# A group's token rows by PE transposes instead of a DRAM round trip, gate stores on ACT's queue, row numbers in one transfer

## The chip, the cores and the metric

The kernel runs on one core of one Trainium2 chip. The metric is the device time of one execution in microseconds (us). PE is the matrix engine, PEld its weight load, DVE the vector engine, ACT the activation engine, POOL the general one. SP only issues transfers. Transfers are issued on the queues of SP, ACT and POOL, and 16 DMA engines carry them all.

## The reference

One layer of a decoder for 256 prompt tokens and 8 sample tokens, D_MODEL = 2048, in float32. Two mixers (a state-space scan and a short convolution) and a layer norm give x1. Then comes a layer of single-neuron experts, 8 heads with the best 16 of 16384 each, a second norm and a gated sum.

```python
def peer(x, w_q, keys1, keys2, u_tab, v_tab):
    ...
    t1, i1 = lax.top_k(s1, PEER_TOPK)
    t2, i2 = lax.top_k(s2, PEER_TOPK)
    ...
    top, pos = lax.top_k(cand, PEER_TOPK)
    idx = jnp.take_along_axis(cand_idx, pos, axis=-1)
    gate = jax.nn.softmax(top, axis=-1)
    ...
        hid = jax.nn.gelu(jnp.einsum('td,thkd->thk', xb, u_tab[ib]).astype(jnp.float32), approximate=False)
        coef = (gb * hid).astype(xb.dtype)
        return jnp.einsum('thk,thkd->td', coef, v_tab[ib])
```

## The kernel before

All activations lie transposed (features on partitions, 264 tokens along the free dimension). Weights stream in halves of a 128-column block (128x1024, 512 KB). SP fetches a half into one of five w buffers (L135), ACT rounds it to whi (L146), DVE takes the rest as wlo (L147), and PE multiplies with both. `next_half` runs the fetch four halves and the split three halves (LOOK = 3) ahead of PE.

The program order is made by a tick after every half. `tick` calls `background`, which runs the functions that `defer` and `soon` have made due and then lets the tasks (generators) issue work up to a budget; a task yields the DVE time it has issued, or ("w", n) to rest n ticks. On the chip each engine and each queue takes its instructions in that order.

After the first norm (x1) and the queries, the experts are done in two ways.

- **208 tokens, dense.** All 16384 experts are multiplied with them on PE: the U stage (`pair_block` with uT, 128 blocks, results evacuated by L1350, L1351, L1354 and stored to a_d on ACT's queue, L1355) and the V stage (vP). `select` (DVE) finds each token's experts. `gates` makes one-hot tiles (L1218 on POOL and DVE, L1219 and L1220 on ACT). `g_mm` multiplies them on PE (L1231), ACT copies the result into gs (L1232), and every 32 tokens gs is stored to g_d (2 MB, 7 stores, the last into gr_d half as long) on SP's queue (L1223). The V stage reads g_d and a_d back.
- **56 tokens, sparse** (x1sp: 48 of the prompt and the 8 of the samples), by gathering the rows of the chosen experts. They are in three groups, GR = 32, 16 and 8 tokens. A tile of 128 partitions holds, for each of its chosen experts, one row of 2048. For group g it has 128/n experts of each of n tokens at a time, so the token's x1 must stand on its 128/n partitions: the tile x1s.

`send` (L1172 on) writes the chosen indices (ix) and gates (sel) to sx_d and sg_d in DRAM, in an order that `index` (L1263, L1264) can read as one column per gather. Prompt tokens (t = 0) go on POOL's queue, 16 transfers of the samples (t = 1) on SP's queue, two ticks after they are made (`later_rows`). `token_rows` transposes the 56 tokens on PE (16 transposes, L1242), copies them out (L1243) and stores each group's rows with 128/n copies to x1_d in DRAM (L1246, 3 stores of 1 MB on POOL's queue, x_d in the profile). `replicate` (L1268) reads a group's 128 rows back into x1s.

`sparse_experts` then runs 112 jobs on a grid of ticks. Each gathers 128 rows (ug, 1 MB, L1257 on POOL) and works on them on DVE: a product with x1s and its sum for uR (L1307), or a weighted sum into x1s for vR (L1317). `folded` sums the partitions of one token by a matmul with the 0/1 matrix fld.

Of the kernel before, what the change touches and what calls it, by code (L numbers as in the profile page):

```python
# [17 lines left out]
D = 2048  # L18
# [34 lines left out]
def hybrid_step(ctx: ExitStack, tc: tile.TileContext, xT, pT, w_in, w_dt, w_bs, w_bc, w_o, w_q, w_pg, w_pp,  # L53
# [1113 lines left out]

    sx_d = [dram.tile([128, n], U32, name=f"sx{g}_d") for g, (_, n) in enumerate(GR)]
    sg_d = [dram.tile([128, n], F, name=f"sg{g}_d") for g, (_, n) in enumerate(GR)]
    x1_d = [dram.tile([128, D], F, name=f"x1{g}_d") for g in range(len(GR))]  # L1170

    def send(sel, t, nh):  # L1172

        sp = P["sp"]
        ix = sp.tile([128, nh * TOPK], U32, name=f"ix{t}")
        fx = sp.tile([128, nh * TOPK], F, name="fx", tag="fx", bufs=1)
        n = TT[t][1]
        ve.scalar_tensor_tensor(fx[:n], sel[:n, 0], 128.0, sel[:n, 1], OP.mult, OP.add)
        ve.tensor_copy(ix[:n], fx[:n])

        def rows(eng, g, tok, src, stride, runs, m):
            for d, x in ((sx_d[g], ix), (sg_d[g], sel[:, 2])):
                eng.dma_start(out=bass.AP(tensor=d.tensor, offset=d.offset + tok * m,
                                          ap=[[m, len(src)], [stride, runs], [1, m]]),
                             in_=x[src.start:src.stop].rearrange("p (c m) -> p c m", m=m))

        if t == 0:
            for g, (k0, m) in enumerate(GR):
                lo = n - (NSP - NS) + k0
                src = range(lo, min(lo + m, n))  # L1190
                if len(src):
                    rows(gp, g, 0, src, m * m, 128 // m, m)
        else:
            g, m = len(GR) - 1, GR[-1][1]

            def later_rows():
                for h in range(PH):
                    rows(sy, g, h * TOPK + m - NS, range(h * NS, h * NS + NS), m * m, TOPK // m, m)
                DONE["sent"] = True

            defer(2, later_rows)
# [3 lines left out]
    def gates(t0, n):  # L1205
        oh = P["oh"]
        grid = Grid()
        for tt in range(t0, t0 + n, 4):
# [13 lines left out]
            if q0 + 4 == tb:  # L1222
                defer(8, lambda gs=gs, b0=b0: sy.dma_start(out=g_d[b0] if b0 < NB else gr_d, in_=gs))  # L1223
# [9 lines left out]

    def token_rows():

        while "x1" not in DONE or later:
            yield ("w", 1)
        xr = lp.tile([128, D], F, name="xr", tag="ug", bufs=2)
        for b in range(4):
            ps = bank("x1t")  # L1240
            for q in range(4):
                te.transpose(ps[:NSP, q * 128:(q + 1) * 128], x1sp[:, 4 * b + q], ident)  # L1242
            ac.copy(xr[:NSP, b * 512:(b + 1) * 512], ps[:NSP])  # L1243
            yield ("w", 1)
        for g, (k0, n) in enumerate(GR):
            gp.dma_start(out=x1_d[g].rearrange("(q n) d -> n q d", n=n),  # L1246
                         in_=xr[k0:k0 + n, None, :].to_broadcast([n, 128 // n, D]))

    def sparse_experts():
# [15 lines left out]

        def replicate(g):
            t = lp.tile([128, D], F, name="x1s", tag="x1s", bufs=2)
            gp.dma_start(out=t, in_=x1_d[g])  # L1268
            return t
# [20 lines left out]
        xr = replicate(0)  # L1290
        yield ("w", 4)
        grid = Grid()
        g = 0
        for i, (tab, k0, n, c) in enumerate(jobs):
            ks = slice(k0, k0 + n)
            if tab is uR and c == k0:
                x1s = xr
            if tab is vR and c == k0 and g + 1 < len(GR):
                while g + 1 == len(GR) - 1 and "sent" not in DONE:
                    yield ("w", 1)  # L1300
                index(g + 1)
                xr = replicate(g + 1)
# [35 lines left out]
    spawn(token_rows())  # L1338
# [223 lines left out]
def _inputs(x_prompt, x_sample, p_prompt, p_sample, state_ssm, state_ssd_conv, state_shortconv,  # L1562
# [35 lines left out]
        fold=np.concatenate([np.tile(np.eye(g[1]), (128 // g[1], 1)) for g in GR], 1).astype(np.float32),  # L1598
# [34 lines left out]
```

## Time and profile before

| what | value |
|---|---|
| three runs | median 2633.68 us, 2633.47 to 2635.28 |
| the profiled execution | 2632.36 us, its span 2630.5 us |
| mean granted clock of PE | 0.993 |
| busy: PE, DVE, ACT, POOL | 98%, 78%, 54%, 24% of the span |
| DMA | 695.29 MB, 264 GB/s over the span |
| DMA queues' share of 16 engines: SP (q1), POOL (q0), ACT (q10) | 58.8%, 16.8%, 2.0% |
| chain that ended last | PE 76%, DMA 9%, DVE 8%, issue 3%, ACT 2% |

The span runs from the first to the last instruction; the time of the execution is 1.9 us longer. PE's busy share is that of modelled ends and overlapping matmuls, so its idle time and its granted clock (1.00 is 2.4 GHz, 0.50 is 1.2 GHz) tell more. The dense blocks of the U stage end between 1147 and 1874 us, those of the V stage between 1878 and 2514.

### The profile page before, as it was taken

To read this page: it belongs to the slowest core of one execution; us is meant where nothing else is said; L and a number is where in the kernel's file an instruction comes from. 1 tells how busy PE (TensorE), PEld (TensorE's weight loads), DVE (VectorE), ACT (ScalarE), POOL (GpSimd) and SP (SyncE) were. 2 spreads that over 40 slices of the span, in tenths; PEclk is the share of its full clock that TensorE was granted. 3 is DMA by queue.
4 is the path that set the end of the run, shared out by engine and by line. 5 is a ranking of instruction groups with operands and counts; after the bars stand their busy time and mean duration, and the time that the engine had idled before them with its cause. 6 is when DMAs were issued, how large, how long until landed. Compare 5 with 4: busy or idle time off the path is not lost.

```text
span 2630.5 us, 49103 instructions
## 1 busy us (share of the span) xinstructions
PE 2572.6 (98%) x18989; PEld 2536.3 (96%) x18989; DVE 2044.0 (78%) x3308; ACT 1425.5 (54%) x2170; POOL 630.5 (24%) x725
## 2 busy tenths in 40 slices
PE   9999999999999999998999999999999999999999
PEld 8999999999999999997989999998999999999999
DVE  8899965556445567897988777677899989989986
ACT  5665533454334445653567777775544444444563
POOL 2232200000000010100148656752222223322210
PEclk9999999999999999999999999999999999999999
DMA  7798755655666665667779999999999999999664
GB/s 237 219 302 272 238 175 177 184 174 182 179 182 180 181 177 178 181 188 197 219 259 347 344 342 353 344 347 382 369 366 358 379 353 364 374 356 371 207 203 132
DMA packets 204378, 695.29 MB, mean 264 GB/s; under 512 B 23616, under 2 KB 61168, under 8 KB 188144
## 3 DMA queue, kind: packets, MB, share of 16 engines
q1 hardware_dynamic: 156512, 509.13, 58.8%
q0 software_dynamic: 29616, 164.98, 16.8%
q10 hardware_dynamic: 18016, 18.06, 2.0%
q8 instruction: 148, 2.42, 0.4%
q14 instruction: 86, 0.70, 0.1%
HBM read 649.46 MB, written 42.61 MB: 263 GB/s over the span
## 4 chain that ended last, share of the span: by engine, by line
PE 76%; DMA 9%; DVE 8%; issue 3%; ACT 2%; POOL 1%; SPq 0%; ACTq 0%; DVEq 0%; POOLq 0%
PE mm L273 18%; PE mm L239 15%; PE mm L237 15%; PE mm L238 15%; PE mm L274 9%; DMA w<-vP 4%; DVE wlo L147 4%; DMA w<-uT 3%; ACT whi L146 1%; PE mm L276 1%; PE gps L1231 1%; POOL o L1218 1%; DVE ug L1307 1%; DVE x1s L1317 1%; DMA ug<-uR,sidx 0%
## 5 line engine op out<-in xcount | busy, mean ns | idle before, releaser
L147 DVE TENSOR_TENSOR wlo<-w,whi 128x1024 fp32r<-128x1024 f32 x916 | 1116.1, 1224 | 441.9 <-ACT whi L146 432.7
L146 ACT CAST whi<-w 128x1024 fp32r<-128x1024 f32 x916 | 958.3, 1049 | 796.2 <-PE mm L238 285.4
L273 PE MATMUL mm<-x,whi 128*128 128x416 f32 x1920 | 604.4, 374 | 14.3 <-ACT whi L146 14.2
L273 PE MATMUL mm<-co,whi 128*128 128x416 f32 x1920 | 587.7, 367 | 0.0
L239 PE MATMUL mm<-x,wlo 128*128 128x264 f32 x1920 | 549.2, 286 | 2.8 <-DVE wlo L147 2.8
L237 PE MATMUL mm<-x,whi 128*128 128x264 f32 x1920 | 549.1, 286 | 0.0
L238 PE MATMUL mm<-x,whi 128*128 128x264 f32 x1920 | 546.6, 285 | 0.0
L274 PE MATMUL mm<-x,wlo 128*128 128x208 f32 x2048 | 518.0, 263 | 20.6 <-DVE wlo L147 20.4
L274 PE MATMUL mm<-co,wlo 128*128 128x208 f32 x2048 | 513.9, 261 | 6.1 <-DVE wlo L147 5.6
L274 PEld LDWEIGHTS mm<-x,wlo 128*128 128x128 f32 x2048 | 396.4, 194 | 30.3 <-DVE wlo L147 29.8
L274 PEld LDWEIGHTS mm<-co,wlo 128*128 128x128 f32 x2048 | 390.4, 191 | 12.5 <-DVE wlo L147 11.8
L273 PEld LDWEIGHTS mm<-x,whi 128*128 128x128 f32 x1920 | 366.9, 191 | 20.9 <-ACT whi L146 16.1
L239 PEld LDWEIGHTS mm<-x,wlo 128*128 128x128 f32 x1920 | 361.8, 188 | 3.3 <-DVE wlo L147 3.2
L273 PEld LDWEIGHTS mm<-co,whi 128*128 128x128 f32 x1920 | 360.9, 188 | 3.6 <-ACT whi L146 0.2
L237 PEld LDWEIGHTS mm<-x,whi 128*128 128x128 f32 x1920 | 362.6, 189 | 1.5 <-issue 1.4
L238 PEld LDWEIGHTS mm<-x,whi 128*128 128x128 f32 x1920 | 362.9, 189 | 0.0
L1218 POOL TENSOR_SCALAR o<-iot,slot,slot 128x128 f32<-128x128 f32 x156 | 213.9, 1377 | 5.8 <-issue 2.9
L1257 POOL DMA_INDIRECT ug<-vR,sidx x56 | 99.2, 1771 | 318.1 <-DVE x1s L1317 268.3
L1257 POOL DMA_INDIRECT ug<-uR,sidx x56 | 92.9, 1660 | 271.5 <-DVE ug L1307 232.2
L1307 DVE SCALAR_TENSOR_TENSOR ug<-ug,x1s 128x2048 f32<-128x2048 f32 x56 | 127.9, 2283 | 3.6 <-DMA ug<-uR,sidx 3.6
L1317 DVE SCALAR_TENSOR_TENSOR x1s<-ug,scf,x1s 128x2048 f32<-128x2048 f32 x53 | 124.3, 2345 | 4.9 <-DMA ug<-vR,sidx 4.9
L840 POOL CAST r1h<-r1gbh 128x2 fp32r<-128x2 f32 x16 | 5.2, 325 | 476.2 <-PE mm L239 476.2
(363 smaller groups left out, 3928.1 us busy)
## 6 DMA issues: line engine op xcount, KB each, us to landing
w<-uT SPq DMA_DIRECT2D x256, 512.0 KB
w<-vP SPq DMA_DIRECT2D x256, 512.0 KB
w<-w_in SPq DMA_DIRECT2D x240, 512.0 KB
w<-w_bc SPq DMA_DIRECT2D x32, 512.0 KB
w<-w_bs SPq DMA_DIRECT2D x32, 512.0 KB
w<-w_o SPq DMA_DIRECT2D x32, 512.0 KB
w<-w_q SPq DMA_DIRECT2D x32, 512.0 KB
w<-w_pg SPq DMA_DIRECT2D x32, 512.0 KB
```

What stands on the lines that cost most here:

```text
L146: ac.copy(hi, w)
L147: ve.tensor_tensor(lo, w, hi.bitcast(F), OP.subtract)
L237: te.matmul(ps, wh, xh[kb], start=(first and q == 0), stop=False)
L238: te.matmul(ps, wh, xl[kb], start=False, stop=False)
L239: te.matmul(ps, wl, xh[kb], start=False, stop=(last and q == n - 1))
L273: te.matmul(ps, hi[:, ws], xp[kb], start=(kb == 0), stop=False)
L274: te.matmul(ps[:, :TD], lo[:, ws], xp[kb][:, :TD], start=False, stop=False)
L276: te.matmul(ps, hi[:, ws], xp[kb], start=False, stop=True)
L1218: (gp if q < 3 else ve).tensor_scalar(o1[:, q], iot, slot[0][:, c], slot[2][:, c], OP.is_equal, OP.mult)
L1257: gp.indirect_dma_start(out=t, out_offset=None, in_=tab, in_offset=bass.IndirectOffsetOnAxis(ap=sidx[:, c:c + 1], axis=0))
L1307: ve.scalar_tensor_tensor(t, t, 1.0, x1s, OP.mult, OP.mult, accum_out=shid[:, c:c + 1])
L1317: ve.scalar_tensor_tensor(x1s, t, scf[:, c:c + 1], x1s, OP.mult, OP.add)
```

## The change

- `token_rows` and x1_d are gone. `replicate` becomes a task: for each quarter of the 2048 features it spreads the group's columns of x1sp on ACT over 128 columns (each token 128/n times; in the last group by one copy for each of 8 heads), rests a tick, transposes the four 128x128 blocks on PE, copies them out on ACT and rests a tick. The first group waits for it; the next ones are spawned where `replicate` was called.
- The order of a group's partitions follows (token first), and the fold matrix with it. The row numbers and gates of a group are written to DRAM as they stand, by one transfer each, all on POOL's queue; the samples' are written when they are made.
- Gate stores go on ACT's queue.

```diff
--- before.py
+++ after.py
@@ -1165,9 +1165,9 @@
         yield from gates(0, PT // 2)
 
 
+
     sx_d = [dram.tile([128, n], U32, name=f"sx{g}_d") for g, (_, n) in enumerate(GR)]
     sg_d = [dram.tile([128, n], F, name=f"sg{g}_d") for g, (_, n) in enumerate(GR)]
-    x1_d = [dram.tile([128, D], F, name=f"x1{g}_d") for g in range(len(GR))]
 
     def send(sel, t, nh):
 
@@ -1178,27 +1178,16 @@
         ve.scalar_tensor_tensor(fx[:n], sel[:n, 0], 128.0, sel[:n, 1], OP.mult, OP.add)
         ve.tensor_copy(ix[:n], fx[:n])
 
-        def rows(eng, g, tok, src, stride, runs, m):
+        for g, (k0, m) in enumerate(GR):
+            if (g + 1 == len(GR)) != (t == 1):
+                continue
+            lo = 0 if t else n - (NSP - NS) + k0
             for d, x in ((sx_d[g], ix), (sg_d[g], sel[:, 2])):
-                eng.dma_start(out=bass.AP(tensor=d.tensor, offset=d.offset + tok * m,
-                                          ap=[[m, len(src)], [stride, runs], [1, m]]),
-                             in_=x[src.start:src.stop].rearrange("p (c m) -> p c m", m=m))
-
-        if t == 0:
-            for g, (k0, m) in enumerate(GR):
-                lo = n - (NSP - NS) + k0
-                src = range(lo, min(lo + m, n))
-                if len(src):
-                    rows(gp, g, 0, src, m * m, 128 // m, m)
-        else:
-            g, m = len(GR) - 1, GR[-1][1]
-
-            def later_rows():
-                for h in range(PH):
-                    rows(sy, g, h * TOPK + m - NS, range(h * NS, h * NS + NS), m * m, TOPK // m, m)
-                DONE["sent"] = True
-
-            defer(2, later_rows)
+                x = x[lo:lo + (n if t else m)]
+                gp.dma_start(out=bass.AP(tensor=d.tensor, offset=d.offset, ap=[[x.shape[1], x.shape[0]], [1, x.shape[1]]]),
+                             in_=x)
+        if t:
+            DONE["sent"] = True
 
     GS = {}
 
@@ -1220,7 +1209,7 @@
             ac.activation(o2, o2, AF.Relu, bias=1.0, scale=-1.0)
             defer(6, lambda o1=o1, o2=o2, gs=gs, q0=q0: g_mm(o1, o2, gs, q0))
             if q0 + 4 == tb:
-                defer(8, lambda gs=gs, b0=b0: sy.dma_start(out=g_d[b0] if b0 < NB else gr_d, in_=gs))
+                defer(8, lambda gs=gs, b0=b0: ac.dma_start(out=g_d[b0] if b0 < NB else gr_d, in_=gs))
             yield 0.1
             yield grid(3)
         DONE["G" + str(t0)] = True
@@ -1230,21 +1219,6 @@
         for q in range(4):
             te.matmul(ps[:, q * 128:(q + 1) * 128], o2[:, q], o1[:, q], start=True, stop=True)
         ac.copy(gs[:, :, q0:q0 + 4].rearrange("p e t -> p t e"), ps.rearrange("p (t e) -> p t e", e=128))
-
-    def token_rows():
-
-        while "x1" not in DONE or later:
-            yield ("w", 1)
-        xr = lp.tile([128, D], F, name="xr", tag="ug", bufs=2)
-        for b in range(4):
-            ps = bank("x1t")
-            for q in range(4):
-                te.transpose(ps[:NSP, q * 128:(q + 1) * 128], x1sp[:, 4 * b + q], ident)
-            ac.copy(xr[:NSP, b * 512:(b + 1) * 512], ps[:NSP])
-            yield ("w", 1)
-        for g, (k0, n) in enumerate(GR):
-            gp.dma_start(out=x1_d[g].rearrange("(q n) d -> n q d", n=n),
-                         in_=xr[k0:k0 + n, None, :].to_broadcast([n, 128 // n, D]))
 
     def sparse_experts():
         jobs = [(tab, k0, n, c) for k0, n in GR for tab in (uR, vR) for c in range(k0, k0 + n)]
@@ -1263,10 +1237,29 @@
             gp.dma_start(out=sidx[:, k0:k0 + n], in_=sx_d[g])
             gp.dma_start(out=scf[:, k0:k0 + n], in_=sg_d[g])
 
+        XR = {}
+
         def replicate(g):
+
+            k0, n = GR[g]
             t = lp.tile([128, D], F, name="x1s", tag="x1s", bufs=2)
-            gp.dma_start(out=t, in_=x1_d[g])
-            return t
+            for b in range(4):
+                tb = t[:, b * 512:(b + 1) * 512]
+                x = x1sp[:, 4 * b:4 * b + 4, k0:k0 + n]
+                if g + 1 < len(GR):
+                    ac.copy(tb.rearrange("p (q i c) -> p q i c", q=4, i=n),
+                            x[:, :, :, None].to_broadcast([128, 4, n, 128 // n]))
+                else:
+                    for h in range(PH):
+                        ac.copy(tb.rearrange("p (q h i c) -> p q h i c", q=4, h=PH, i=NS)[:, :, h],
+                                x[:, :, :, None].to_broadcast([128, 4, n, TOPK // NS]))
+                yield ("w", 1)
+                ps = bank("x1t")
+                for q in range(4):
+                    te.transpose(ps[:, q * 128:(q + 1) * 128], tb[:, q * 128:(q + 1) * 128], ident)
+                ac.copy(tb, ps)
+                yield ("w", 1)
+            XR[g] = t
 
         def folded(g, acc):
 
@@ -1287,19 +1280,18 @@
         yield ("w", 1)
         index(0)
         get(0)
-        xr = replicate(0)
-        yield ("w", 4)
+        yield from replicate(0)
         grid = Grid()
         g = 0
         for i, (tab, k0, n, c) in enumerate(jobs):
             ks = slice(k0, k0 + n)
             if tab is uR and c == k0:
-                x1s = xr
+                x1s = XR.pop(g)
             if tab is vR and c == k0 and g + 1 < len(GR):
                 while g + 1 == len(GR) - 1 and "sent" not in DONE:
                     yield ("w", 1)
                 index(g + 1)
-                xr = replicate(g + 1)
+                spawn(replicate(g + 1))
             get(i + 1)
             yield grid(STEP - (i % (4 if vp else 2) == 0))
             t = rows.pop(i)
@@ -1335,7 +1327,6 @@
     ctx.push(sp_stack)
     ctx.push(oh_stack)
     slot = [tp.tile([128, TD], F, name=f"slot{q}") for q in range(3)]
-    spawn(token_rows())
     spawn(select_all())
 
 
@@ -1595,7 +1586,8 @@
         eye=np.eye(128, dtype=np.float32),
         tri=np.triu(np.ones((128, 128), np.float32)),
         iota=np.tile(np.arange(128, dtype=np.float32), (128, 1)),
-        fold=np.concatenate([np.tile(np.eye(g[1]), (128 // g[1], 1)) for g in GR], 1).astype(np.float32),
+        fold=np.concatenate([np.repeat(np.eye(n), 128 // n, 0) for _, n in GR[:-1]]
+                            + [np.tile(np.repeat(np.eye(NS), TOPK // NS, 0), (PH, 1))], 1).astype(np.float32),
     )
```

**SP's queue.** Before, with the weights w counted where they follow each other; these are the last two of the samples' sixteen transfers and the first gate stores (one piece of the difference):

```order
-L1183 DMA sx_d<-ix_16283 8x2x8
-L1183 DMA sg_d<-sel_16075 8x2x8
-L135 DMA w<-uT 128x1024 x24
-L1223 DMA g_d<-gs 128x4096
-L135 DMA w<-uT 128x1024 x22
-L1223 DMA g_d<-gs 128x4096
-L135 DMA w<-uT 128x1024 x13
-L1223 DMA gr_d<-gs 128x2048
-L135 DMA w<-uT 128x1024 x25
```

All of it is gone: the 256 uT weights now stand in one row, with nothing between them.

**POOL**, from the keys' loads to the first gather (o are the one-hots of a gate). Before:

```order
L1013 DMA keys<-keysT 128x256 x8
L1246 DMA x_d<-xr 32x4x2048
L1246 DMA x_d<-xr 16x8x2048
L1246 DMA x_d<-xr 8x16x2048
L1183 DMA sx_d<-ix_16010 32x4x32
L1183 DMA sg_d<-sel_15353 32x4x32
L1183 DMA sx_d<-ix_16010 16x8x16
L1183 DMA sg_d<-sel_15353 16x8x16
L1218 TENSOR_SCALAR o_16105<-iot,slot_14375,slot_14377 128x128 x3
```

Now:

```order
L1013 DMA keys<-keysT 128x256 x8
L1187 DMA sx_d<-ix_15979 32x128
L1187 DMA sg_d<-sel_15322 32x128
L1187 DMA sx_d<-ix_15979 16x128
L1187 DMA sg_d<-sel_15322 16x128
L1207 TENSOR_SCALAR o_16074<-iot,slot_14372,slot_14374 128x128 x3
L1207 TENSOR_SCALAR o_16182<-iot,slot_14372,slot_14374 128x128 x3
L1187 DMA sx_d<-ix_16252 64x16
L1187 DMA sg_d<-sel_16044 64x16
L1207 TENSOR_SCALAR o_16295<-iot,slot_14372,slot_14374 128x128 x3
```

The three stores of token rows are gone, and the samples' two transfers stand between the second and the third gate.

**ACT** in the U stage, at the first group's second quarter, as it is now (in as the hidden values of the dense experts are made):

```order
L1341 COPY as<-mm 128x208
L1221 COPY gs<-gps 128x4x128
L1250 COPY x1s<-x1sp 128x512
L1208 ACTIVATE o_16413<-iot,slot_14373 128x128 x4
L1209 ACTIVATE o_16413<-o_16413 128x512
L146 CAST whi<-w 128x1024
L1345 ACTIVATE as<-as 128x416
L1346 DMA a_d<-as 128x416
L1260 COPY x1s<-x1t 128x512
L146 CAST whi<-w 128x1024
```

The spreading copy and the copy out of PSUM are new there, each between two casts of weights; the four transposes stand on PE between them.

## Rows read from the trace of the kernel before

**Rows 1.** The page: busy us of each engine (share of the span) xinstructions.
```profile
PE 2572.6 (98%) x18989; PEld 2536.3 (96%) x18989; DVE 2044.0 (78%) x3308; ACT 1425.5 (54%) x2170; POOL 630.5 (24%) x725
```

**Rows 2.** Stretches: us, busy (xinstructions) of PE PEld DVE ACT POOL, PEclk, DMA share, GB/s.
```profile
1210.00:1220.00 10.00, 10.00 (x70) 9.88 (x70) 9.65 (x33) 5.71 (x8) 1.74 (x3) 1.00 0.91 210
1225.00:1280.00 55.00, 39.90 (x206) 36.28 (x204) 36.07 (x102) 17.55 (x24) 0.00 (x0) 0.81 0.71 198
1330.00:1345.00 15.00, 11.95 (x61) 11.16 (x60) 8.75 (x31) 8.20 (x17) 4.12 (x5) 0.77 0.91 344
1345.00:1370.00 25.00, 22.60 (x156) 22.15 (x155) 23.70 (x63) 18.45 (x31) 4.92 (x4) 1.00 0.66 209
```

**Rows 3.** PE's timeline: start, us, line, operation; in brackets the idle time before.
```profile
1229.29 0.37 PE L273 MATMUL mm<-x,whi 128*128 128x416 f32 x1
...
1234.25 0.71 PE L273 MATMUL mm<-x,whi 128*128 128x416 f32 x1 [4.18 <-ACT whi L146]
...
1235.85 0.59 PE L273 MATMUL mm<-x,whi 128*128 128x416 f32 x1
```

**Rows 4.** DMA, 1210 to 1250: queue, packets, MB, share of 16 engines; issues.
```profile
q0 software_dynamic: 560, 3.15, 50.9%
...
x_d<-xr POOLq DMA_DIRECT2D x3, 1024.0 KB
```

**Rows 5.** Chain of waits, 1165 to 1360: start, us, what.
```profile
1219.53 29.39 DMA w<-uT
```

**Rows 6.** Stretches, columns as in rows 2: selection stage, and before it.
```profile
1223.62:1367.03 143.41, 122.86 (x745) 117.68 (x744) 112.69 (x288) 75.36 (x120) 25.45 (x26) 0.90 0.72 219
1193.14:1223.62 30.48, 30.48 (x208) 29.87 (x208) 29.03 (x98) 16.65 (x25) 1.74 (x3) 1.00 0.78 190
```

**Rows 7.** SP's timeline, 1300 to 1420: first small transfer, next weight.
```profile
1326.17 0.35 SPq L1183 DMA_DIRECT2D sx_d<-ix  x1
...
1336.54 56.36 SPq L135 DMA_DIRECT2D w<-uT  x24
```

**Rows 8.** SP's waits, whole span: us in total, times, longest.
```profile
SPq L1223 <- ACT gs L1232: 22.4, 5, 6.0
...
SPq L1223 <- ACT as L1354: 10.5, 2, 6.0
...
SPq L1183 <- DVE ix L1179: 5.0, 1, 5.0
```

**Rows 9.** Stretches behind the seven gate stores: first, last, sum (columns of rows 2).
```profile
1400.00:1430.00 30.00, 27.05 (x185) 26.29 (x184) 22.09 (x30) 20.91 (x36) 19.71 (x16) 1.00 0.95 357
...
1780.00:1810.00 30.00, 28.01 (x174) 26.96 (x172) 19.78 (x20) 15.35 (x24) 7.64 (x9) 0.94 1.01 398
sum 160.00, PE 149.72 PEld 143.77 DVE 114.62 ACT 111.90 POOL 78.02; mean PE 21.39 PEld 20.54 DVE 16.37 ACT 15.99 POOL 11.15
```

**Rows 10.** Reads of x1s: its issues (1656 to 1690, then tile); stretches behind.
```profile
x1s<-x_d POOLq DMA_DIRECT2D x1, 1024.0 KB
...
L1268 POOL DMA_DIRECT2D x1s<-x_d x3: 544/558/605, 1326.6 to 2136.4; - x3
...
1680.00:1700.00 20.00, 18.12 (x115) 17.65 (x114) 13.09 (x13) 12.98 (x23) 12.89 (x8) 0.91 0.95 357
2150.00:2170.00 20.00, 18.21 (x115) 16.67 (x114) 16.17 (x18) 10.41 (x11) 2.53 (x2) 1.00 0.86 325
```

**Rows 11.** Chain of waits, 1165 to 1360: four transposes.
```profile
1203.06 0.44 PE x1t L1242 x4
```

**Rows 12.** ACT by tile or line: ns min/median/max, first and last start, forms.
```profile
L1243 ACT COPY xr<-x1t x4: 575/579/580, 1178.3 to 1210.9; 56x512 f32<-56x512 f32 x4
...
L1232 ACT COPY gs<-gps x52: 1052/1134/1181, 1325.8 to 1772.0; 128x512 f32<-128x512 f32 x52
...
L1133 ACT ACTIVATE sel<-sel x3: 216/311/313, 1304.2 to 1486.7; 128x128 f32<-128x128 f32 x2, 64x16 f32<-64x16 f32 x1
```

**Rows 13.** ACT in a stretch: length, busy (xinstructions), PEclk, DMA share, GB/s.
```profile
1300.00:1330.00 30.00, 23.31 (x38) 1.00 0.70 211
```

## The prediction

> **What bounds the kernel now.** I read the page's busy shares first: PE is busy for 2572.6 of the span of 2630.5 us [rows 1], so nearly every gain has to be a microsecond in which PE idles, or runs at its lower clock. I then cut the span into stretches to see where that happens. A clean stretch of the U stage shows 70 matmuls in 10 us, PE busy throughout, granted clock 1.00. The worst one, 1225 to 1280 us, shows 206 in 55 us and a clock of 0.81 [rows 2]: 55 less 39.90 busy is 15.1 us idle, and 55 x 0.19 = 10.4 us goes to the clock, 25.5 together. By count the same comes out: (385 - 206) / 7 per us = 25.6. The timeline there shows the cause of both: PE waits 4.18 us for a whi, and before the wait a 416-column matmul takes 0.37 us, behind it 0.59 [rows 3], so the engine that had idled goes on at 1.2 instead of 2.4 GHz.
>
> What is late is a weight. The chain of waits has one weight transfer under way for 29.39 us [rows 5]. In those 40 us the POOL queue holds the 16 DMA engines for 50.9% of their time with 3.15 MB, which are the three x_d stores of 1 MB [rows 4]: the token rows, written to DRAM 128 rows at a time.
>
> Two smaller losses follow. From 1330 to 1345 us 3.05 us are idle and 15 x 0.23 = 3.45 go to the clock, 6.5 together; from 1345 to 1370 another 2.4 are idle [rows 2]. There the SP queue, which carries the weights, first waits 5.0 us for the sample tokens' indices (DVE ix) [rows 8] and then issues sixteen small transfers, from 1326.17 to 1336.54 [rows 7]. Later the same queue stands 22.4 + 10.5 us over seven times before a gate store, because ACT has not yet filled gs [rows 8], and 2 MB then go ahead of the next weight.
>
> **The change part by part.** The sum is against the profiled execution, 2632.36 us; the median of the three runs, 2633.68, is 1.3 above it, inside what such runs scatter.
>
> *Token rows off DRAM, sample row numbers off SP: the stretch 1223.62 to 1367.03.* It lasts 143.41 us with 745 matmuls [rows 6]. At 70 in 10 us they need 106.4, the floor for PE. But DVE is busy for 112.69 us in it [rows 6], and its order hardly changes: the selection of the experts and the wlo halves stand as before. So DVE is late next. In the stretch before, it is busy 29.03 of 30.48 us, 95%, while PE stands at no time [rows 6]; at that share 112.69 us of work take 118. Against that, split_w runs three halves ahead (LOOK), some 7 us at most, of which I take 4 as in hand when the stretch begins, and where it is pressed DVE works without gaps. Ends: 106.4 (PE alone) and 118 (DVE at 95%, no lead). I take 112, close to DVE's own 112.69: **-31 us** (between -37 and -25). The selection keeps the rest of the loss.
>
> *Gate stores on ACT's queue.* In the seven stretches behind the stores PE is busy 149.72 of 160 us, and the last, at clock 0.94, gives 30 x 0.06 = 1.8 more [rows 9]: 12.1 us is the most that can come back. The bytes stay, so the least is 0; 2 MB at the 357 GB/s of such a stretch hold the engines 5.9 us whoever issues them. What goes is SP's wait ahead of them, 32.9 us in total, about 4.7 a store, in which no weight is asked for and the five w buffers run dry. I take two thirds, **-8 us**, nearer the upper end because waits of that length are what turns a 6 us transfer into a stall. The Trainium skill (DMA: Bandwidth & Descriptors, Issuing engines are not separate DMA queues) speaks against this: transfers started from different engines share the same 16 DMA engines, and another queue saves only issue time. By that rule this term is 0 and the sum 8 us higher; it does not speak of a queue that waits in order, and rows 8 show one.
>
> *Reads of the replicated rows.* Three reads of 1 MB go. The second, issued between 1656 and 1690, and the last, at 2136.4, are each followed by a loss [rows 10]: 1.88 idle + 20 x 0.09 = 3.7 us at 1680 to 1700, and 1.79 at 2150 to 2170, 5.5 in all. Gathers and weights fill the queues there too, so between 0 and 5.5; I take **-2.5**. The first read lies in the stretch already counted.
>
> *Transposes.* 48 of 128x128 come for 16 of 56 rows. Four take 0.44 us of PE's path [rows 11]; twelve fours less four fours are 8 x 0.44 = **+3.5 us**, all on the path.
>
> *ACT.* For the first two groups, 8 spreading copies and 8 evacuations of 128x512; an evacuation of 56x512 takes 579 ns, the strided gs copy of 128x512 1134 [rows 12], so a spreading copy costs 0.58 to 1.13. I take 0.65: 16 copies, 9.8 us. The last group's 32 copies of 64 elements are priced by the smallest activation, 216 ns [rows 12], 6.9 us, and its 4 evacuations add 2.3. Four xr copies (2.3) go. Seven issues of 0.35 us [rows 7] come over. Some +19 us on an engine that is 78% busy where the gates begin (23.31 of 30) [rows 13]. Its work lies beside PE's, except at one place: PE takes a transpose in order, one tick (a half block: 16 matmuls, 2.3 us at 70 in 10) after its spreading copy is issued. Whenever ACT is later than that, PE waits with the weights ready. Eight such places come while gates are being made: 0 if ACT keeps up, 8 x 1.2 = 10 if it is half a tick late each time. Idle at 22% says it mostly keeps up: **+3 us**. In the V stage I cost the small copies at nothing, hidden under waits for weights; without that cover they would be 6.9 us.
>
> *At no cost.* The sample row numbers go to POOL, behind two gates: POOL now stands for ix, and the next gate's one-hots wait behind it, but their matmuls are due six ticks later, some 14 us, against a wait of the order of SP's 5.0 [rows 8]. The sparse chain starts six ticks later (eight short steps instead of one wait of four) and, by the order, its last fold comes one tick later, with the final statistics at the same place. The fold and the index layout change numbers, not instructions.
>
> Sum: -31 - 8 - 2.5 + 3.5 + 3 = -35: **2597 us**.
>
> **The rivals.**
> - *DVE and ACT take the gain back in the selection stage* (0.20). If whi comes late because ACT carries the spreading copies, DVE, which follows it, cannot use its lead: the stretch takes 122 instead of 112, the stores bring 4: -21 - 4 - 1 + 3.5 + 3 = -19.5, 2613. For: DVE at 95% before the stretch. Against: it works without gaps when pressed.
> - *The stores bring nothing* (0.18). The DMA engines are busy at 0.95 in the first of those stretches and at 1.01 in the last [rows 9]; a 2 MB burst then delays the weights whatever queue it is on. All else as forecast: 2605. Against: the seven waits of rows 8. The Trainium skill's rule (DMA: Bandwidth & Descriptors, Issuing engines are not separate DMA queues) would give this case.
> - *Everything comes back* (0.12): DVE's lead covers the selection, and the stores and reads give their upper ends: -36 - 12 - 5.5 + 3.5 = -50, 2582.
> - *ACT's queue turns against PE* (0.04): slower. The stores of the hidden values (a_d) share the queue now and stand behind 2 MB. Their tile has two buffers, so a store must land within about five halves, 12 us, or ACT's next evacuation waits, and with it whi and PE. 2 MB need 5.9 us alone, twice that at half the bandwidth, 18 at a third. At a third ACT would wait 6 us seven times, 42 us, and the time would be 2639. It decides from 17 us a store: 36 / 7 = 5.2 us of waiting each eats the whole gain. For it: three queues are loaded at once. Against: with five w buffers in hand the weights ask for little at first, and ACT has 22% to spare.
>
> That the change does not do what it says I leave out: SP's row of 256 uT weights is unbroken in the new order, and no x_d is left.
>
> **How the numbers follow.** Forecast 0.46, the rivals 0.20, 0.18, 0.12, 0.04. The bounds of the terms reach from -37 - 12.1 - 5.5 + 3.5 = -51 (2581) to -25 + 3.5 + 10 = -11.5 (2621). The range 2583 to 2617 leaves out half of the third rival, the fourth and the far end of the first. Faster by over 0.2% (5.3 us, about what a measurement of this kernel tells from no change): 0.94, all cases but the fourth less 0.02 for a chain of small mishaps, which is the chance of no change; slower 0.04.
>
> **What would show it.** Right: no x_d; 1225 to 1280 at clock 1.00 with PE busy almost throughout; DVE at 9.5 or more of 10 from 1225 to 1340, and the longest PE waits there on wlo, not on weights; SP with no wait on gs; PE waits on x1s copies of some 3 us in total. Wrong in the first term: a weight still under way for over 15 us near 1220. Wrong in the second: stalls of 1 to 3 us some 10 us behind each store on ACT's queue. The fourth rival: ACT's evacuations waiting for a_d. The forecast as a whole is wrong if PE's idle time falls by less than 12 us.

## The result, and the profile after

The changed kernel takes 2600.48 us (median of 4 runs, 2599.55 to 2606.2) beside 2633.81 us for the kernel before on the same chip: a ratio of 0.9877, with a 95% interval of 0.986 to 0.9894, so 33 us faster (28 to 37). The forecast was 2597 us, 2583 to 2617. Its profiled execution took 2601.0 us, with a span of 2598.9. The same kernel measured a second time: ratio 0.986 (0.9845 to 0.9875). Its executions there lie between 2597.97 and 2607.48, so totals that differ by a few us say little; the stretches say more.

The page of the changed kernel, busy times and ACT's queue:
```profile
PE 2561.6 (99%) x19021; PEld 2530.9 (97%) x19021; DVE 2041.5 (79%) x3308; ACT 1438.2 (55%) x2218; POOL 614.3 (24%) x721
...
q10 hardware_dynamic: 19024, 31.69, 3.3%
```
PE idles 37.3 us (span less busy time) instead of 57.9 [rows 1], and its mean granted clock is 0.998 instead of 0.993, which over the span is some 13 us; the two together are about the gain. The gate stores' bytes stand on q10, ACT's queue.

Stretches of the changed kernel (columns as in rows 2):
```profile
1225.00:1280.00 55.00, 51.85 (x330) 50.40 (x329) 53.38 (x126) 26.47 (x36) 0.00 (x0) 0.97 0.67 209
1225.00:1370.00 145.00, 139.27 (x921) 136.86 (x920) 135.62 (x317) 100.40 (x164) 45.34 (x39) 0.98 0.74 236
1300.00:1345.00 45.00, 42.42 (x287) 41.73 (x286) 40.11 (x118) 38.04 (x63) 21.66 (x21) 0.96 0.75 234
1330.00:1345.00 15.00, 15.00 (x107) 14.76 (x106) 14.49 (x36) 11.83 (x20) 5.27 (x4) 1.00 0.83 256
1345.00:1370.00 25.00, 25.00 (x175) 24.88 (x174) 24.33 (x31) 21.19 (x38) 15.54 (x8) 1.00 0.86 299
```
The same long stretch of the kernel before:
```profile
1225.00:1370.00 145.00, 124.45 (x754) 119.26 (x753) 114.55 (x290) 77.93 (x123) 28.42 (x28) 0.91 0.73 223
```
In the 145 us from 1225 to 1370 there are 921 matmuls where there were 754. At the 6.8 a us of a stretch without gaps (985 in the same 145 us, in an experiment below) the 167 more are 24.6 us. 1330 to 1370, where 8.9 us were lost [rows 2], has no gap left. What is still lost lies at two places: 1225 to 1280 (3.15 us idle, 55 x 0.03 = 1.65 of clock, against 25.5), and 1300 to 1345 (2.58 idle and 45 x 0.04 = 1.8).

What holds the DMA engines from 1210 to 1250 now (columns as in rows 4):
```profile
q1 hardware_dynamic: 1887, 6.88, 58.0%
...
w<-uT SPq DMA_DIRECT2D x14, 512.0 KB
```
POOL's queue, which had 50.9% of them [rows 4], has nothing there; fourteen weights are asked for in these 40 us, where there were eight.

PE's longest waits of the kernel before, whole span (us in total, times, longest):
```profile
PE mm L274 <- DVE wlo L147: 26.0, 34, 2.7
PE mm L273 <- ACT whi L146: 14.2, 5, 6.3
```
Those of the changed kernel:
```profile
PE mm L274 <- DVE wlo L147: 13.5, 20, 2.7
PE x1t L1259 <- ACT x1s L1250: 4.7, 3, 2.6
PE pil L871 <- DVE x1sp L1275: 1.7, 1, 1.7
```
The 14 us that PE stood for a whi are gone. The new wait is x1t, the transposes that stand for ACT's spreading copy. The longest of these on PE's timeline, and ACT's timeline ahead of it, which shows why the copy is late:
```profile
1311.80 1.11 PE L1259 MATMUL x1t<-ident,x1s 128*128 128x128 f32 x4 [2.58 <-ACT x1s L1250]
```
```profile
1302.41 1.28 ACT L1133 ACT_TABLE_LOAD   x1
...
1305.87 1.28 ACT L1345 ACT_TABLE_LOAD   x1
...
1308.12 1.28 ACT L1208 ACTIVATE o<-iot,slot 128x128 f32<-128x128 f32 x4 [0.40 <-ACT as L1345]
...
1309.97 1.03 ACT L146 CAST whi<-w 128x1024 fp32r<-128x1024 f32 x1
...
1311.13 0.62 ACT L1250 COPY x1s<-x1sp 128x512 f32<-128x512 f32 x1
```
Two activation tables are loaded, 1.28 us each, one for the selection's Exp and one back for the hidden values; a gate's one-hots and a whi follow, and only then, at 1311.13, the copy for which PE has stood since 1309.22. That the loads are what makes it late is read from this order; no run took them away, and at the second group, where PE stands 2.1 us at x1t between 1660 and 1705, no table is loaded.

### The profile page after: what moved, and what is told of

Its sections match the earlier page's. It is cut to its first block, busy times and chain, and to the rows that moved or that the text cites. A ratio compares the mean times of both kernels' runs of the same rounds, so it can differ in the third digit from the quotient of the medians.

```text
span 2598.9 us, 49190 instructions
## 1 busy us (share of the span) xinstructions
PE 2561.6 (99%) x19021; PEld 2530.9 (97%) x19021; DVE 2041.5 (79%) x3308; ACT 1438.2 (55%) x2218; POOL 614.3 (24%) x721
## 4 chain that ended last, share of the span: by engine, by line
PE 77%; DMA 8%; issue 6%; DVE 5%; ACT 4%; SPq 0%; ACTq 0%; POOL 0%; DVEq 0%; POOLq 0%
PE mm L273 19%; PE mm L239 14%; PE mm L237 14%; PE mm L238 14%; PE mm L274 10%; DMA w<-uT 4%; DVE wlo L147 2%; DMA w<-vP 2%; ACT whi L146 2%; PE mm L276 1%; PE gps L1220 1%; ACT o L1208 1%; DMA w<-w_in 1%; DVE ug L1299 1%; PE yS L1270 0%
## 5 line engine op out<-in xcount | busy, mean ns | idle before, releaser
L273 PE MATMUL mm<-x,whi 128*128 128x416 f32 x1920 | 595.5, 370 | 0.0
L1207 POOL TENSOR_SCALAR o<-iot,slot,slot 128x128 f32<-128x128 f32 x156 | 197.6, 1273 | 12.4 <-issue 9.4
```

The source lines that it names most:

```text
L273: te.matmul(ps, hi[:, ws], xp[kb], start=(kb == 0), stop=False)
L1207: (gp if q < 3 else ve).tensor_scalar(o1[:, q], iot, slot[0][:, c], slot[2][:, c], OP.is_equal, OP.mult)
```

## The experiments

All ratios are to the kernel before, run beside them on the same chip.

### What starved the weights at 1220: the bytes, the queue, or the detour

One run stores each token row once and lets the read replicate it; the other moves the same three stores to ACT's queue.
```diff
 e3_before_rows_once (kernel before)
-            gp.dma_start(out=x1_d[g].rearrange("(q n) d -> n q d", n=n),
-                         in_=xr[k0:k0 + n, None, :].to_broadcast([n, 128 // n, D]))
+            gp.dma_start(out=x1_d[g][0:n], in_=xr[k0:k0 + n])
-            gp.dma_start(out=t, in_=x1_d[g])
+            d = x1_d[g]
+            gp.dma_start(out=t, in_=bass.AP(tensor=d.tensor, offset=d.offset,
+                                            ap=[[0, 128 // GR[g][1]], [D, GR[g][1]], [1, D]]))
 e4_before_rows_actq (kernel before)
-            gp.dma_start(out=x1_d[g].rearrange(...
+            ac.dma_start(out=x1_d[g].rearrange(...
```


> The kernel before with each token row stored once (56 rows, 0.46 MB, instead of 384 rows, 3.1 MB) and replicated by the reads, whose bytes stay. Theory (the bytes of the three stores hold the DMA engines and starve the weights): the loss at 1225 to 1280 us falls from 25.5 to the some 5 us that the changed kernel still loses there, so -20 us (-24 to -15), about 2613; the longest weight transfer there falls from 29 us to under 12. Rival (the transposes, the evacuations or the detour itself make the stall): no change, 2632.

> The kernel before with the same three 1 MB stores issued on ACT's queue instead of POOL's. Theory (bytes): the weight is starved as before, 0 us within 6, 2627 to 2640. Rival (it is POOL's queue, whose packets hold the engines longer per byte): most of the 20 us come back, about 2613.

Measured: rows once 1.0021 (1.0009 to 1.0033), 5 us slower where 20 faster were expected; on ACT's queue 0.9992 (0.998 to 1.0004), no change. By its total the first run speaks for the rival; its stretches do not:
```profile
1225.00:1280.00 55.00, 52.24 (x334) 51.09 (x334) 53.38 (x126) 26.61 (x36) 0.00 (x0) 0.97 0.69 210
1300.00:1345.00 45.00, 31.48 (x185) 30.00 (x184) 25.95 (x85) 24.02 (x40) 9.89 (x12) 0.85 0.65 196
1640.00:1740.00 100.00, 84.83 (x565) 82.33 (x564) 60.73 (x68) 67.48 (x120) 53.91 (x41) 0.93 0.87 301
```
From 1225 to 1280 it has 334 matmuls against 206 [rows 2] and as many as the changed kernel: with the bytes down to 0.46 MB the starved weight is gone, though the transposes, the evacuations and POOL's queue are as before. (The packets of POOL's queue fall with the bytes, from 560 [rows 4] to 112, so these two were not told apart.) The loss comes back elsewhere, 13.5 us idle from 1300 to 1345 and 15.2 from 1640 to 1740. These are the places of the reads. PE's waits, and SP's timeline at the first place:
```profile
PE mm L274 <- DVE wlo L147: 35.8, 34, 13.1
PE mm L273 <- ACT whi L146: 13.3, 3, 9.0
```
```profile
1305.15 0.35 SPq L1183 DMA_DIRECT2D sx_d<-ix  x1
...
1323.33 20.29 SPq L135 DMA_DIRECT2D w<-uT  x9
```
SP's sixteen small transfers, issued in 10.4 us before [rows 7], take until 1323.33, 18.2 us, before the next weight; PE then stands 9.0 us for a whi and, behind the second read, in the stretch from 1640, 13.1 for a wlo. That read is 16 rows fetched eight times each:
```profile
x1s<-x_d POOLq DMA_DIRECT2D x1, 1024.0 KB, 18.4
```
It lands after 18.4 us. All three reads of this run, and the three of 128 separate rows in the run with the gate stores on ACT's queue (below), by time to landing:
```profile
DMA to landing us min/median/max: 12.3/18.4/22.1
DMA to landing us min/median/max: 6.5/6.9/8.9
```
The same edit thus shows both: fewer bytes stored cure the first stall, and a read of few rows many times lands late and makes others. Behind the read of 128 separate rows at the second place PE idles 1.88 us [rows 10]. The run on ACT's queue leaves the stall as it was:
```profile
1225.00:1280.00 55.00, 34.61 (x180) 31.18 (x180) 34.76 (x101) 16.19 (x23) 0.00 (x0) 0.78 0.68 175
```
```profile
q10 hardware_dynamic: 671, 3.52, 58.6%
...
x_d<-xr ACTq DMA_DIRECT2D x3, 1024.0 KB
```
So which queue issues the stores is not the cause; here the stores hold the engines 58.6% of the time, as POOL's did 50.9% [rows 4].

### The sample row numbers: SP's wait, or the sixteen transfers

```diff
 e5_after_numbers_sp (changed kernel)
-                gp.dma_start(out=bass.AP(...), in_=x)
+                dst = bass.AP(...)
+                if t:
+                    defer(2, lambda dst=dst, x=x: sy.dma_start(out=dst, in_=x))
+                else:
+                    gp.dma_start(out=dst, in_=x)
 ...     (DONE["sent"] is deferred by the same two ticks)
```


> The changed kernel with the last group's row numbers on SP's queue, in two transfers. Theory (the loss at 1330 to 1345 came from sixteen issues that stood among the POOL queue's transfers): two transfers cost nothing, 0 within 2 us against the changed kernel, ratio 0.986 to 0.987. Rival (it came from SP's wait of 5.0 us for the indices, with the weights behind it): +3 to +6 us, ratio 0.988 to 0.989, and PE waits for a weight some 15 us behind that wait.

Measured: 0.9861 (0.9842 to 0.9879), between the two ratios of the changed kernel; an interval of this width does not exclude 3 us, so the trace decides. SP's wait and the stretch:
```profile
SPq L1189 <- DVE ix L1179: 5.0, 1, 5.0
```
```profile
1300.00:1345.00 45.00, 42.40 (x297) 41.77 (x296) 41.36 (x121) 39.57 (x69) 21.84 (x18) 1.00 0.76 246
```
SP stands its 5.0 us again with the weights behind it [rows 8], and PE has 297 matmuls in a stretch where the changed kernel has 287; its only gap there is the 2.60 us at x1t. So this wait of 5 us of the queue in order cost nothing that can be seen. What cost the 6.5 us at 1330 was the sixteen transfers among POOL's traffic, or the read that they met; two transfers with no read beside them cost nothing. Those two were not separated.

### What is left in the selection stage: DVE, or ACT ahead of the transposes

```diff
 e6_after_spread_early (changed kernel; for b in range(7), spread b, transpose b - 3)
-                yield ("w", 1)
-                ps = bank("x1t")
+                if b > 2:
+                    tb = t[:, (b - 3) * 512:(b - 2) * 512]
+                    ps = bank("x1t")
 e7_after_pace (changed kernel)
             ve.max_index(i[:, 8:16], a[:, 8:16], cf)
-            yield 0.95
+            yield 1.65 if nh > 1 else 0.95
 e8_both: both edits; e9_after_again: the changed kernel
```


> The changed kernel with each spreading copy three ticks ahead of its transposes, in the same eight ticks a group. Theory (PE takes the transposes in order and ACT reaches the spreading copy late: PE stands 4.7 us at x1t): these waits go, -4 us against the changed kernel (between -5.5 and -1), about 2597. Rival (ACT is the limit of that stretch itself, so that PE stands for whi or wlo instead): 0 within 1.5 us, and the idle time moves to other names.

> The changed kernel with the planner's price of the selection's five scans of one head raised from 0.95 to 1.65, so that about one tick in four or five gets none of them. Theory (DVE is late next: scans of 1.64 us and a wlo of 1.2 are more than the 2.4 us of a half, and its lead is gone at 1240): the 3.15 us of idle and 1.7 us of low clock at 1240 to 1260 go, -4 us (between -5 and -2), about 2597. Rival (the selection only ends later, and the gates and the V stage with it): 0 to +3.

> Both edits in one kernel. Theory: -8 us against the changed kernel (between -10 and -4), about 2593, with PE at no wait of over 1.5 us between 1190 and 1370. Rival (one limit takes over from the other): no better than the better of the two alone, about 2597.

> The changed kernel itself, unedited, as the base for the three others of this call on the same chip: 2600 to 2602. Against it the kernel with the gate stores back on SP's queue (2601.6 by its own call) tells whether that part is worth the 8 us of the prediction or 0 to 2.

Measured: spread early 0.9845 (0.983 to 0.986), pace 0.9844 (0.983 to 0.9857), both 0.983 (0.9815 to 0.9845), the changed kernel 0.986 (0.9845 to 0.9875); medians 2598.57, 2594.72, 2595.0 and 2602.25 us. The intervals overlap, so the totals alone do not rank them. The long stretch of the early spread, then PE's waits in it:
```profile
1225.00:1370.00 145.00, 138.99 (x922) 135.53 (x922) 136.26 (x318) 99.23 (x164) 43.02 (x39) 0.99 0.73 237
```
```profile
PE mm L274 <- DVE wlo L147: 5.9, 4, 2.7
```
The x1t wait is gone from this stretch and PE does no more matmuls than before the edit (922 against 921, and 926 in the second profile of the changed kernel): a wait of 2.6 us on a wlo, between 1325 and 1345, has come in its place. Here the rival was right. At the second group the theory was: from 1640 to 1740 PE is busy for all of the 100 us, with 699 matmuls where both profiles of the changed kernel have 680. That is 2.8 us, and the total (2598.57 against 2602.25) lies where the theory put it. The pace edit:
```profile
1225.00:1370.00 145.00, 145.00 (x985) 143.77 (x984) 133.40 (x308) 104.12 (x169) 37.86 (x38) 1.00 0.76 243
```
PE is busy for all of the 145 us at full clock, with 985 matmuls, and no wait of PE is left in the stretch, not even the one at x1t; at the second group 2.1 us of them remain. DVE's busy time in it is 133.40, less than the 135.62 of the changed kernel; the work was only spread. The groups on DVE in the changed kernel from 1225 to 1255 show what pressed (line, operation, xcount | busy us, mean ns | idle):
```profile
L147 DVE TENSOR_TENSOR wlo<-w,whi 128x1024 fp32r<-128x1024 f32 x10 | 12.0, 1211 | 0.0
L1095 DVE MAX8 top<-cand 128x8 f32<-128x112 f32 x8 | 2.2, 278 | 0.3
...
L1094 DVE MATCH_REPLACE8 cand<-top,cand 128x112 f32<-128x112 f32 x8 | 2.1, 260 | 0.0
...
L1094 DVE MATCH_VALUE_LOAD cand<-top,cand 128x8 f32 x8 | 0.7, 93 | 0.3
```
Five scans of 0.26 to 0.28 us and their three loads of 0.09 are 1.6 us a head, entered in the planner as 0.95; with a wlo of 1.2 that is 2.8 us in a half block of 2.4. Eight heads in a row take the lead that split_w had. With the lead kept, ACT's lateness at 1309 is covered too. The two edits together do 986 matmuls there, and their median is 2595.0 against 2594.72 for the pace alone: no better than the better of the two, as the rival had it. Theirs is the lowest ratio, 7 us under the changed kernel measured beside it, and the intervals just meet. The pace edit gave PE 8.7 us in this stretch ((985 - 926) / 6.8) against the second profile of the changed kernel; its total is 4 us lower by the ratios and 7.5 by the medians. Some of the gain is lost again in the last 150 us, where PE's wait on acc is 3.1 us instead of 2.1 and PE idles 10.4 us instead of 8.0, and to scatter.

### The gate stores and the reads: two losses or one

```diff
 e1_before_gates_act (kernel before); e2_after_gates_sp and e12_after_gates_sp_again: the reverse, in the changed kernel
-                defer(8, lambda gs=gs, b0=b0: sy.dma_start(out=g_d[b0] if b0 < NB else gr_d, in_=gs))
+                defer(8, lambda gs=gs, b0=b0: ac.dma_start(out=g_d[b0] if b0 < NB else gr_d, in_=gs))
 e10_before_one_read (kernel before); e11_before_one_read_gates_act: with the edit of e1 besides
+            if g == 0:
                 gp.dma_start(out=t, in_=x1_d[g])
+            else:
+                k0, n = GR[g]
+                for b in range(4):
+                    ac.copy(t[:, b * 512:(b + 1) * 512].rearrange("p (q i c) -> p q i c", q=4, i=n),
+                            x1sp[:, 4 * b:4 * b + 4, k0:k0 + n, None].to_broadcast([128, 4, n, 128 // n]))
```


> Theory (SP's in-order waits of 32.9 us ahead of seven gate stores are what loses PE time): the gate stores alone bring -8 us against the kernel before (between -12.1 and -4), all of it behind the stores between 1370 and 1820 us; SP's waits on ACT gs are gone. Rival (the stores bring nothing, the transfers share the same DMA engines): 0, within 2 us, with PE stalls of the same size behind each store.

> The same part undone in the changed kernel. Theory: +8 us against the changed kernel (2608 to 2609), SP again waits some 30 us on ACT gs. Rival (the stores bring nothing, the U stage gained by something else): 0, within 2 us, 2600 to 2602.

> The changed kernel with the gate stores back on SP's queue, a second time and beside the two others, since scatter between executions is some 3 us. Theory (shared loss, already back with the reads gone): 0 to +4 us against the changed kernel, ratio to the kernel before 0.986 to 0.988. Rival (the stores are worth 8 to 12 us here too): ratio 0.989 or more.

> The kernel before without the second and third 1 MB read of replicated rows (the rows of these two groups are filled by four copies on ACT from the columns, so these samples' outputs are not the reference's). Theory (gate stores and these reads share one loss, which either edit can bring back): -6 us against the kernel before (-9 to -4), more than the 2.5 of the prediction. Rival (the two terms are separate): -2.5 us (-4 to 0).

> The same with the gate stores on ACT's queue besides. Theory (one shared loss): the second edit adds only -2 to -5 us to the first, in all -10 us (-13 to -7), not more than the gate stores alone brought (-12). Rival (separate): -14.5 us, the -12 of the gate stores alone and the -2.5 of the reads.

Measured, as us against the kernel before: gate stores on ACT's queue alone 0.9955 (0.994 to 0.997), -12, which the theory allowed and the rival of no gain did not; two reads fewer 0.9969 (0.9955 to 0.9984), -8; both 0.9945 (0.9924 to 0.9965), -14.5 (-20 to -9). The -14.5 is the number of the rival, separate terms with 2.5 us for the reads; but the reads gave 8, and separate terms would then give -20, the end of the interval. By the totals the question stays open.

In the changed kernel, the stores back on SP: 0.9867 (0.9848 to 0.9886) and 0.9887 (0.9868 to 0.9907). The second lies between the theory's range and the rival's. Their mean is 0.9877 against 0.9869 for the two measurements of the changed kernel, which is 2 us; against the run with the row numbers on SP, measured beside the second (2600.33 us), that one is 5 us slower. So the same edit brought 12 us in the kernel before (8 to 16), and 2 to 5 in the changed one, where the rival came and the scatter does not exclude 0.

The stretch of the gates, 1370 to 1820: the kernel before, then its three edits in the order stores, reads, both:
```profile
1370.00:1820.00 450.00, 437.62 (x2954) 429.54 (x2954) 346.42 (x398) 335.15 (x572) 276.28 (x198) 0.99 0.93 349
1370.00:1820.00 450.00, 441.88 (x3010) 434.58 (x3009) 352.71 (x406) 339.81 (x577) 275.68 (x202) 1.00 0.96 357
1370.00:1820.00 450.00, 440.63 (x2989) 433.36 (x2988) 349.78 (x401) 341.43 (x582) 280.12 (x199) 1.00 0.94 350
1370.00:1820.00 450.00, 442.07 (x3017) 435.43 (x3015) 352.68 (x406) 343.03 (x583) 274.23 (x200) 1.00 0.95 354
```
Against the 2954 matmuls of the kernel before they have 56, 35 and 63 more. Separate losses would give 91, so 28 are counted twice. Where, the stretch behind the second read shows, of the first two edits:
```profile
1680.00:1700.00 20.00, 20.00 (x140) 19.89 (x139) 15.31 (x16) 15.94 (x27) 10.74 (x8) 1.00 0.99 384
1680.00:1700.00 20.00, 20.00 (x140) 19.90 (x138) 16.39 (x17) 16.43 (x29) 14.96 (x10) 1.00 0.97 374
```
With 115 matmuls before [rows 10], either edit has 25 more there: the gap behind the read goes with the read, and it goes (but for 0.70 and 0.97 us at 1667 and 1670) with the gate stores off SP's queue, though the read stays. No gate store is near it: before, SP issues them at 1633.63 and 1706.12, and PE stands at 1689.42. Why it needs both the traces do not tell. The gaps behind the later stores are another loss, which the reads do not touch. With two reads fewer PE stands 0.96 us at 1658.76, 0.72 at 1728.18 and 1.20 at 1785.39; before it stood 0.97, 0.72 and 1.01 at these places. At 1415, ahead of both reads that were taken out, it stands 0.94 us where it stood 2.29, so that part of the 35 is scatter.

The same stretch in the changed kernel, as it is and with the stores back on SP (the second run):
```profile
1370.00:1820.00 450.00, 439.98 (x2987) 431.17 (x2986) 344.95 (x393) 337.77 (x573) 246.11 (x190) 1.00 0.95 353
1370.00:1820.00 450.00, 437.93 (x2965) 428.11 (x2964) 340.44 (x388) 335.05 (x568) 254.54 (x190) 1.00 0.94 351
```
The other profiles of these two kernels have 2998 and 2972, so the stores' queue is worth some 24 matmuls here, 3.5 us, where it was worth 56, 8.2 us, in the kernel before. These are one or two profiles each, and two of one kernel differ by some 10. SP's wait for the seven stores (the half one into gr_d is the third of them) is as long in the changed kernel with the stores on SP as it was before, 30.8 us against 32.9 [rows 8]:
```profile
SPq L1212 <- ACT gs L1221: 30.8, 7, 5.3
```
So the wait alone does not set the loss.

The V stage has no gate store in it. From 1820 to 2430, the kernel before and the one with two reads fewer:
```profile
1820.00:2430.00 610.00, 602.81 (x3980) 592.03 (x3979) 543.51 (x551) 291.99 (x307) 170.30 (x152) 1.00 0.97 366
1820.00:2430.00 610.00, 605.36 (x4010) 596.88 (x4010) 549.28 (x556) 295.77 (x311) 167.34 (x152) 1.00 0.97 366
```
These 30 matmuls, 4.5 us, can't be put down to the third read: the runs that keep it have 4005 (gate stores on ACT's queue) and 4002 (token rows on ACT's queue), and the changed kernel has 4041 in one profile and 3990 in the other. This stage scatters by as much as it gained, and no run shows what the third read costs.

## Why the prediction came out right

The sum, -35, lies between the two measurements (-32 and -37 by their ratios), and the likeliest case is the one that came. Its terms did not all come out, and that their errors cancel is in part luck: the first stretch gave 24.6 us and everything else 8 to 12, where the sum had 31 and 4.

*The stretch 1223.62 to 1367.03, -31.* The cause was right: the x_d stores (rows once cures the stall, another queue does not). So was the next limit: DVE is late at 1240, with a wlo as PE's longest wait there, 3.15 us idle and 1.65 of clock, 4.8 in all against the 5.6 that the choice of 112 us over the floor of 106.4 left; and the pace edit, which only spreads DVE's work, removes it. That "where it is pressed DVE works without gaps" held from 1225 to 1280 (53.38 of 55 us) but not from 1300 to 1345 (40.11 of 45), where ACT brings the copies late. The stretch gave 24.6 us, not 31. Of the difference 4.4 is the wait at x1t and the clock behind it, which the sum has under ACT. The rest comes from the floor: a stretch without gaps runs 6.8 matmuls a us and not the 7 that I took from ten clean microseconds, so 745 of them need 109.6 us.

*ACT, +3.* Right in kind, too low: 4.7 us at x1t over both groups, 2.6 of it in one wait, and 1.8 of clock behind that one. The prices were near (a spreading copy takes 0.61 us where I took 0.65). What I left out is the two table loads of 1.28 us, which stand ahead of the first group's copies. And the term is no property of ACT alone: with three ticks of distance the wait at the first group turned into one on a wlo, and with DVE's lead kept it vanished there.

*Gate stores, -8, and reads, -2.5.* The sum of the two, 10.5, lies inside what both edits give together (9 to 20 us; 63 matmuls, 9.3 us, in the stretch of the gates). The reasons were not right. The step that failed is "SP's wait ahead of them, 32.9 us in total, about 4.7 a store, in which no weight is asked for and the five w buffers run dry". The same wait stood in the changed kernel with the stores on SP, 30.8 us, and in the run with the row numbers on SP, 5.0 us, at a cost of 2 to 5 us and of nothing: weights in hand cover most of such a wait. In the kernel before, the edit is worth 8.2 us by its matmuls (12 by its total), but 25 of those 56 matmuls, 3.7 us, are the gap behind the second read, the very 3.7 that I had in the reads' term. So either edit brings that loss back, and it can't be counted for both. What remains of the stores' term once the reads are gone, some 3.5 us, is less than half of the 8. The rule that spoke against this term (the Trainium skill, DMA: Bandwidth & Descriptors, Issuing engines are not separate DMA queues) comes near the 2 to 5 us of the changed kernel, and does not agree with the 12 us (8 to 16) that the same edit brought in the kernel before.

*Transposes, +3.5.* Four take 0.44 us in the kernel before [rows 11]; no run shows by itself what the added ones cost.

*At no cost.* One item may have had a price: PE stands 1.7 us for x1sp before the last statistics where it stood 0.4. That the sparse chain's last fold, a tick later, is the reason was not tested.

*The rivals.* The forecast left 5.6 us over the floor in the first stretch, and the rival in which DVE and ACT take the gain back left 15.6. The changed kernel still loses 9.2 there (4.8 at 1240, 4.4 at 1309), so this rival held for about a third, and the time is far from its 2613. That the stores bring nothing is nearly true of the changed kernel, where some 3.5 of the 8 us are left; the time, 2600 to 2602, lies between the forecast and this rival's 2605. ACT's queue did not turn against PE: no wait of ACT for an a_d is in its list.

## What to carry to other kernels

Look for the transfer that is under way while a weight is late, and change its bytes before its queue: three stores of 1 MB starved the weights from either queue. A queue that waits in order is not yet a loss; ask how long the buffers behind it last. And one loss can stand in two terms, if either of two edits removes it: undo each edit in the new kernel, not only in the old, before giving each its microseconds. Last, check a planner's prices against the trace once a stall in front of them is gone (five scans entered as 0.95 us took 1.6 and were the next 4 to 9 us).

## What the runs showed of the hardware

The stores of the token rows were dear by the byte: 3.15 MB held 50.9% of sixteen engines for 40 us [rows 4], 103 engine-us a MB, and on ACT's queue, with 0.4 MB of other stores, 58.6% for 3.52 MB, 107. The weights took 44 in the same 40 us of the kernel before, and 54 in the changed kernel (58.0% for 6.88 MB). The replication alone does not explain it: stored once, the rows still took 83. The weights before, then the rows stored once, from 1210 to 1250:
```profile
q1 hardware_dynamic: 1106, 4.03, 27.4%
q0 software_dynamic: 112, 0.46, 6.0%
```

The reads of 1 MB that repeat a few rows landed after 22.1 us (32 rows four times), 18.4 (16 rows eight times) and 12.3 (8 rows sixteen times), those of 128 separate rows after 6.5 to 8.9. The read with the most repeats landed soonest of its three, and the traffic beside each differs; why they are slow the traces do not tell.
